# Low parts by a product with minus the identity, LayerNorm and block sums moved between engines

## The chip, the cores and the metric

One core of a Trainium2 chip runs the whole layer. The metric is the device time of one execution, in microseconds (us); lower is better. The kernel before takes 1218.13 us, the median of three runs (1217.9 to 1218.59).

## The reference

One decoder layer on 1024 tokens of width 1024, in float32:

```python
h = layer_norm(x, ln_in_g, ln_in_b)
proj = h @ w_in                       # q, k, v of two groups of 8 heads, 64 wide
sb = stick_breaking_attention(...)    # group 0, all earlier keys
sw = sliding_window_attention(...)    # group 1, last 128 keys, sinks, bias
merged = concat([rms_norm(sb, g0), rms_norm(sw, g1)])
h = layer_norm(ALPHA * h + merged @ w_out, ln1_g, ln1_b)
h = layer_norm(ALPHA * h + swiglu_ffn(h), ln2_g, ln2_b)
```

ALPHA is 2 to the power 1/4. An RMSNorm divides by a root mean square over 512 columns.

## The kernel before, in words

**Precision.** TensorE (PE) multiplies in a short float32 format (`fp32r`). Each operand is therefore split into a high part, rounded to that format, and a low part, the rest, and a product is three matmuls (`mm3`, L149). `split_w` (L105) splits what lies in SBUF: the high part on ScalarE (ACT), the low part by a subtraction on GpSimd (POOL). `split_ps` (L109) splits what lies in PSUM: the high part on ACT, the low part by a subtraction on VectorE (DVE), since POOL does not read PSUM.

**Stages, by the times of the profile.** The entry (0 to some 57 us): `entry(t)` (L282) normalizes the 8 tiles of 128 tokens, transposes each in two groups of four blocks into PSUM (tag `tr`, two banks), splits them into `xh` and `xl`, multiplies the tile by ALPHA and stores it to `h_dram` over ACT's DMA queue; the first projections and the first blocks of sliding-window attention run between the tiles. Then projections and attention, merged head pair by head pair, to some 489 us. Beside the last pair's attention (from some 385 us) run the four chunks of the first half of the output projection, `c1_steps` (L575), for the sliding-window group. From 489 to 574 us the second half runs for the other group: for each chunk `out_load` (L484) loads 512 rows by 256 tokens, splits them with `split_w` and forms squares on ACT and their sums over four blocks on POOL (L491, L492); `out_proj` (L495) sums the rest over the partitions by a product with ones (`pr`, L501), takes the power minus one half on POOL, and for each token tile runs 24 matmuls of 512 columns, which DVE scales and adds to `res` (L510); then `ln_apply` (L628) and `put_b` (L608), which transposes and splits tiles of 512 columns into the right operands of the feed-forward part (B11, B21 for the tokens of the first half; for those of the second half B22, T2, T3, T1, T4, which are sums and differences of blocks as in Strassen's scheme, L638 to L641). The chunks go in the order 0, 2, 1, 3. From 574 us the feed-forward part runs, with PE busy to the end.

**LayerNorm.** `ln_apply` (L128) has two forms. The fast one is three DVE instructions after the statistics (L131, and L134 twice). The other subtracts the mean on ACT (L141), multiplies on DVE (L142) and adds the bias on POOL (L144), each in two halves. The fast form serves tiles 0 to 2 of the entry and tile 7 of the second LayerNorm. The power for `rstd` is on POOL in both (L115).

**Order.** The order of each engine's queue is fixed when the program is built: the framework simulates the program and issues, on each engine, the ready instruction of the highest priority, program order first. An engine then works through its queue in that order. The DMA queue of SyncE (SP) carries all loads and the `h1_dram` stores.

## Time and profile before

| what | value |
|---|---|
| median of three runs | 1218.13 us |
| the profiled execution, its own time | 1216.92 us |
| its span, first to last instruction | 1215.1 us |
| PE / DVE / POOL / ACT busy share | 94% / 70% / 54% / 47% |
| mean granted TensorE clock | 0.974 |
| instructions | 17655 |

A group's row gives busy time, mean time of one instruction and the idle time of the engine just before, with what ended it. A wait names the engine that waited, the instruction that released it, the total, the number of times and the longest. A row of a timeline gives start, duration, engine, line, operation and tiles (output, arrow, inputs). PE is busy 94% over all, so the 6% in which it is not are in a few stretches, and those are looked at one by one.

### The profile page before, as it was taken

What the parts mean: (1) busy time and instruction counts of PE and PEld (TensorE: products, weight loads), DVE (VectorE), ACT (ScalarE), POOL (GpSimd) and SP (SyncE); (2) the same over time, 40 slices, a digit from 0 to 9 for tenths busy, and PEclk for the clock granted to TensorE, in tenths of its full rate; (3) what the DMA queues carried; (4) which work ended last, traced back from release to release, by engine and by line L of the source; (5) the groups of instructions that cost most, each with busy time, mean ns of one, the idle gap of its engine ahead of it and who ended that gap; (6) DMA issues with size and microseconds to landing.
All of it is one profiled execution on the core that took longest, in us unless ns stands there. A gap on an engine that the chain in (4) does not pass through costs nothing. (4 is left out here: it accounts for less than half of the span.)

```text
span 1215.1 us, 17655 instructions
## 1 busy us (share of the span) xinstructions
PE 1138.8 (94%) x6246; PEld 984.6 (81%) x6246; DVE 852.9 (70%) x1319; ACT 572.5 (47%) x1224; POOL 655.0 (54%) x620
## 2 busy tenths in 40 slices
PE   5698999999999898877999999999999999999997
PEld 3588999899998786765888888888888888888885
DVE  7876787788889896578765555555655438899735
ACT  4565677777768565233423322233222325445531
POOL 5614344566557875576886566665666612000584
PEclk9899999999999799987999999999999999999999
DMA  7213102020104635132333234332332239964431
GB/s 278 94 51 101 36 23 76 25 66 22 50 19 152 197 116 184 67 140 104 131 138 95 80 112 130 100 99 78 116 127 96 87 105 365 344 188 110 136 122 69
DMA packets 60053, 140.68 MB, mean 116 GB/s; under 512 B 7060, under 2 KB 18877, under 8 KB 59966
## 3 DMA queue, kind: packets, MB, share of 16 engines
q1 hardware_dynamic: 45406, 110.71, 28.4%
q10 hardware_dynamic: 14560, 28.85, 6.2%
q8 instruction: 49, 0.80, 0.3%
q14 instruction: 38, 0.31, 0.1%
HBM read 95.75 MB, written 41.17 MB: 113 GB/s over the span
## 5 line engine op out<-in xcount | busy, mean ns | idle before, releaser
L107 POOL TENSOR_TENSOR w<-s,w 128x512 fp32r<-128x512 f32 x88 | 123.6, 1407 | 120.1 <-ACT w L106 120.1
L154 PE MATMUL pp<-xh,whi 128*128 128x256 f32 x544 | 158.0, 291 | 0.5 <-DVE q L316 0.5
L154 PE MATMUL pp<-xh,wlo 128*128 128x256 f32 x544 | 156.9, 289 | 0.0
L154 PE MATMUL pp<-xl,whi 128*128 128x256 f32 x544 | 156.3, 287 | 0.0
L106 ACT CAST w<-s 128x512 fp32r<-128x512 f32 x88 | 54.4, 621 | 203.2 <-PE pgu L703 117.7
L776 PE MATMUL pd<-bhl,ahl 128*128 128x512 f32 x612 | 139.2, 389 | 0.0
L776 PEld LDWEIGHTS pd<-bhl,ahl 128*128 128x128 f32 x612 | 114.8, 188 | 24.2 <-DVE bhl L768 0.4
L735 DVE TENSOR_TENSOR t<-t,pgu 128x512 f32<-128x512 f32 x88 | 60.1, 683 | 96.2 <-PE pgu L703 95.9
L433 POOL TENSOR_TENSOR s<-s,s 128x127 f32<-128x127 f32 (+2 forms) x96 | 92.5, 968 | 37.7 <-DVE s L429 33.3
L154 PEld LDWEIGHTS pp<-xh,whi 128*128 128x128 f32 x544 | 105.5, 194 | 1.1 <-PE trx L290 0.6
L154 PEld LDWEIGHTS pp<-xh,wlo 128*128 128x128 f32 x544 | 105.3, 194 | 1.2
L154 PEld LDWEIGHTS pp<-xl,whi 128*128 128x128 f32 x544 | 105.4, 194 | 1.0
L768 POOL TENSOR_TENSOR ahl<-ar,ahl 128x512 fp32r<-128x512 f32 x12 | 16.2, 1354 | 134.8 <-ACT ahl L767 134.7
L429 DVE TENSOR_TENSOR_SCAN s<-s,brk 128x128 f32<-128x128 f32 (+1 forms) x64 | 74.8, 1175 | 11.3 <-ACT s L420 10.8
L110 ACT CAST at<-tra 128x256 fp32r<-128x256 f32 (+1 forms) x160 | 55.6, 356 | 53.1 <-DVE at L111 30.6
L767 ACT CAST ahl<-ar 128x512 fp32r<-128x512 f32 x63 | 39.1, 622 | 76.2 <-PE pd L776 48.8
L374 POOL TENSOR_TENSOR L<-L,rd 128x512 f32<-128x512 f32 (+1 forms) x32 | 30.9, 987 | 79.9 <-DVE rd L372 62.3
L111 DVE TENSOR_TENSOR at<-tra,at 128x256 fp32r<-128x256 f32 (+1 forms) x160 | 58.6, 383 | 18.3 <-ACT at L110 17.1
L107 POOL TENSOR_TENSOR w<-gr,w 128x512 fp32r<-128x512 f32 x44 | 61.1, 1402 | 2.0 <-ACT w L106 2.0
L703 PE MATMUL pgu<-B11h,w 128*128 128x512 f32 x176 | 59.3, 399 | 1.1 <-ACT w L106 1.1
L703 PE MATMUL pgu<-T4h,w 128*128 128x512 f32 x176 | 57.9, 390 | 0.0
L703 PE MATMUL pgu<-B22h,w 128*128 128x512 f32 x176 | 57.8, 389 | 0.0
(222 smaller groups left out, 3325.4 us busy)
## 6 DMA issues: line engine op xcount, KB each, us to landing
ar<-a_dram SPq DMA_DIRECT2D x73, 256.0 KB, 3.0
a_dram<-act ACTq DMA_DIRECT2D x33, 512.0 KB, 2.6
gr<-in_w_gu SPq DMA_DIRECT2D x24, 512.0 KB, 3.7
ur<-in_w_gu SPq DMA_DIRECT2D x23, 512.0 KB, 3.5
bq<-in_w_down SPq DMA_DIRECT2D x44, 256.0 KB, 5.2
raw<-in_w_sb SPq DMA_DIRECT2D x12, 512.0 KB, 3.5
h_dram<-x ACTq DMA_DIRECT2D x8, 512.0 KB, 3.5
m<-o_dram SPq DMA_DIRECT2D x32, 128.0 KB, 3.0
```

Source lines behind the costliest of these rows:

```text
L106: act.copy(hi, raw)
L107: pool.tensor_tensor(out=lo, in0=raw, in1=_f(hi), op=ALU.subtract)
L110: act.copy(hi, ps)
L111: dve.tensor_tensor(out=lo, in0=ps, in1=_f(hi), op=ALU.subtract)
L154: pe.matmul(ps, a, b, start=(i == 0), stop=(i == n - 1))
L374: pool.tensor_tensor(out=Ls[i], in0=Ls[i], in1=rd[:, 2 * i:2 * i + 2].unsqueeze(2).broadcast_to([P, 2, nk]), op=ALU.mult)
L429: dve.tensor_tensor_scan(s2[:, 0:w][:, ::-1], s2[:, 0:w][:, ::-1], brk[:, 512 - w:][:, ::-1] if last else zero.broadcast_to([P, w]), 1.0 i ...
L433: pool.tensor_tensor(out=s1[:, 0:m], in0=s1[:, 0:m], in1=s2[:, 1:m + 1], op=ALU.mult)
L703: pe.matmul(ps, a, b, start=(start and n == 0), stop=(stop and n == 11), skip_group_check=True)
L735: add = lambda out, x: dve.tensor_tensor(out=out, in0=x, in1=ps, op=ALU.add)
L767: act.copy(w[:, 0], src)
L776: pe.matmul(pd[t], x, y, start=(first and k == 0 and n == 0), stop=(end and k == KF - 1 and n == 2), skip_group_check=True)
```

## The change

The low part of a transposed operand is made in PSUM: the transposes are left open as an accumulation group, ACT copies the high part out, PE multiplies the high part by minus the identity into the same bank, and ACT copies what is left as the low part (`split_pe`). The product and the second copy of one split are issued after the transposes and first copy of the next (`pending`, `flush`). This serves the entry (16 splits) and `put_b` (28 calls; T4 in two halves, so 32 splits). From the tenth `put_b` on the transposes take turns between the PSUM tags `tr` and `av`. In `out_load` the low part goes from POOL to DVE, and the POOL sums go: four products with ones take the place of one. ALPHA is folded into the RMS factor and the epsilon, so that the entry's ACT pass over the tile goes. Entry tile 2 takes the slow form of LayerNorm, all tiles of the second LayerNorm the fast one. The sums and differences of `h` (L638, L639, L641) go from POOL to DVE. The entry's weight is loaded as one row and spread by a product with ones, as its bias is already, in place of a broadcast DMA.

```diff
@@ -90,6 +90,8 @@
     ident = cst.tile([P, P], F32, name="ident")
     make_identity(nc, ident)
+    negi = cst.tile([P, P], F32R, name="negi")
+    act.mul(negi, ident, -1.0)
     mhalf = cst.tile([P, 1], F32, name="mhalf")
     dve.memset(mhalf, -0.5)
     ones = cst.tile([P, 1], F32, name="ones")
@@ -110,11 +112,29 @@
         act.copy(hi, ps)
         dve.tensor_tensor(out=lo, in0=ps, in1=_f(hi), op=ALU.subtract)
+    def turn(ps, i, src):
+
+        pe.matmul(ps[:, i, :], src, ident, start=(i == 0), stop=False, is_transpose=True, skip_group_check=True)
+
+    def split_pe(pending, ps, hi, lo):
+
+        act.copy(hi, ps)
+
+        def finish():
+            pe.matmul(ps, negi, hi, start=False, stop=True, skip_group_check=True)
+            act.copy(lo, ps)
+        flush(pending)
+        pending.append(finish)
+
+    def flush(pending):
+        while pending:
+            pending.pop()()
+
     def rpow(dst, var, scale, eps):
         dve.tensor_scalar(out=var, in0=var, scalar1=scale, scalar2=eps, op0=ALU.mult, op1=ALU.add)
         pool.tensor_tensor(out=dst, in0=var, in1=mhalf, op=ALU.pow)
-    def ln_stats(xt, n=2):
+    def ln_stats(xt, n=2, eps=LN_EPS):
         bst = st.tile([P, n, 6], F32, tag=f"bst{n}", name="bst")
         w = D // n
         for i in range(n):
@@ -122,11 +142,11 @@
         mv = st.tile([P, 2], F32, tag="mv", name="mv")
         dve.bn_aggr(out=mv, in_=bst)
         rstd = st.tile([P, 1], F32, tag="rstd", name="rstd")
-        rpow(rstd, mv[:, 1:2], 1.0, LN_EPS)
+        rpow(rstd, mv[:, 1:2], 1.0, eps)
         return mv[:, 0:1], rstd
-    def ln_apply(dst, xt, g, b, fast=False):
-        mu, rstd = ln_stats(xt)
+    def ln_apply(dst, xt, g, b, fast=False, eps=LN_EPS):
+        mu, rstd = ln_stats(xt, 2, eps)
         if fast:
             dve.scalar_tensor_tensor(out=dst, in0=xt, scalar=mu, in1=g, op0=ALU.subtract, op1=ALU.mult)
             for i in range(2):
@@ -234,19 +254,20 @@
             sp.dma_start(xts[t][:, h], x[t * P:(t + 1) * P, h])
-    row = U([1, D], "row", F32)
-    sp.dma_start(row, ln_in[1].unsqueeze(0))
+    rows = [U([1, D], "row", F32) for i in range(2)]
+    for i in range(2):
+        sp.dma_start(rows[i], ln_in[i].unsqueeze(0))
     load_x(0)
     g_in = U([P, D], "g_in", F32)
     b_in = U([P, D], "b_in", F32)
-    bc_load(g_in, ln_in[0])
     load_x(1)
-    row1 = cst.tile([1, P], F32, name="row1")
+    row1 = bb.tile([1, P], F32, tag="oT", name="row1")
     dve.memset(row1, 1.0)
-    for h in (slice(0, 512), slice(512, D)):
-        ps = bps.tile([P, 512], F32, tag="pp", name="bc")
-        pe.matmul(ps, row1, row[:, h], start=True, stop=True)
-        act.copy(b_in[:, h], ps)
+    for i, dst in enumerate((g_in, b_in)):
+        for h in (slice(0, 512), slice(512, D)):
+            ps = bps.tile([P, 512], F32, tag=("pp", "av")[i], name="bc")
+            pe.matmul(ps, row1, rows[i][:, h], start=True, stop=True)
+            act.copy(dst[:, h], ps)
     sink = cst.tile([P, 8], F32, name="sink")
     nsink = cst.tile([P, 8], F32, name="nsink")
     sp.dma_start(sink, sinks.unsqueeze(0).broadcast_to([P, 8]))
@@ -281,15 +302,15 @@
     def entry(t):
         xt = xts.pop(t)
-        ln_apply(xt, xt, g_in, b_in, t < 3)
-        c, o = t // 2, (t % 2) * P
+        ln_apply(xt, xt, g_in, b_in, t < 2)
+        c, o, todo = t // 2, (t % 2) * P, []
         for g in range(2):
             ps = bps.tile([P, 4, P], F32, tag="tr", name="trx")
             for i in range(4):
                 k = 4 * g + i
-                pe.transpose(ps[:, i, :], xt[:, k * P:(k + 1) * P], ident)
-            split_ps(ps, xh[c][:, 4 * g:4 * g + 4, o:o + P], xl[c][:, 4 * g:4 * g + 4, o:o + P])
-        act.mul(xt, xt, ALPHA)
+                turn(ps, i, xt[:, k * P:(k + 1) * P])
+            split_pe(todo, ps, xh[c][:, 4 * g:4 * g + 4, o:o + P], xl[c][:, 4 * g:4 * g + 4, o:o + P])
+        flush(todo)
         act.dma_start(h_dram[t], xt)
     def xmul(w, c0, nc_):
@@ -486,11 +507,10 @@
         for i in range(4):
             sp.dma_start(m[:, i, :], o_dram[4 * g + i][:, c * 256:(c + 1) * 256])
         mh, ml = w_tiles((P, 4, 256))
-        split_w(m, mh, ml)
+        act.copy(mh, m)
+        dve.tensor_tensor(out=ml, in0=m, in1=_f(mh), op=ALU.subtract)
         act.activation(m, m, AF.Square)
-        pool.tensor_tensor(out=m[:, 0:2], in0=m[:, 0:2], in1=m[:, 2:4], op=ALU.add)
-        pool.tensor_tensor(out=m[:, 0], in0=m[:, 0], in1=m[:, 1], op=ALU.add)
-        return mh, ml, m[:, 0]
+        return mh, ml, m
     def out_proj(c, m, wo, acc):
         mh, ml, ss = m
@@ -498,9 +518,12 @@
             t = 2 * c + i
             tok = slice(i * P, (i + 1) * P)
             pr = bps.tile([P, 1], F32, tag="pp", name="pr")
-            pe.matmul(pr, ss[:, tok], ones, start=True, stop=True)
+            for k in range(4):
+                pe.matmul(pr, ss[:, k, tok], ones, start=(k == 0), stop=(k == 3))
             var = st.tile([P, 1], F32, tag="var", name="var")
-            dve.tensor_scalar(out=var, in0=pr, scalar1=1.0 / 512, scalar2=RMS_EPS, op0=ALU.mult, op1=ALU.add)
+
+            dve.tensor_scalar(out=var, in0=pr, scalar1=ALPHA ** 2 / 512, scalar2=ALPHA ** 2 * RMS_EPS,
+                              op0=ALU.mult, op1=ALU.add)
             r = st.tile([P, 1], F32, tag="r", name="r")
             pool.tensor_tensor(out=r, in0=var, in1=mhalf, op=ALU.pow)
             for d in range(2):
@@ -605,17 +628,20 @@
     t4 = [ws.tile([P, 2, 512], F32R, tag="raw", bufs=2, name="T4h") for i in range(2)]
     B["T4"] = (([(t4[0], 0), (t4[1], 2)], [t4[k // 2][:, k % 2] for k in range(4)]), btile(tl, "T4l"))
+    todo = []
+
+    turns = []
+
     def put_b(name, src, o):
-        ps = bps.tile([P, 4, P], F32, tag="tr", name="trh")
+        turns.append(name)
+        ps = bps.tile([P, 4, P], F32, tag="tr" if len(turns) < 10 else ("tr", "av")[len(turns) % 2], name="trh")
         for i in range(4):
-            pe.transpose(ps[:, i, :], src[:, i * P:(i + 1) * P], ident)
+            turn(ps, i, src[:, i * P:(i + 1) * P])
         (hw, _), (lw, _) = B[name]
         for hi, k0 in hw:
             n = hi.shape[1]
-            act.copy(hi[:, :, o:o + P], ps[:, k0:k0 + n])
-            dve.tensor_tensor(out=lw[0][0][:, k0:k0 + n, o:o + P], in0=ps[:, k0:k0 + n],
-                              in1=_f(hi[:, :, o:o + P]), op=ALU.subtract)
+            split_pe(todo, ps[:, k0:k0 + n], hi[:, :, o:o + P], lw[0][0][:, k0:k0 + n, o:o + P])
     order = (0, 2, 1, 3)
     ms = {c: out_load(0, c) for c in order[:2]}
@@ -625,7 +651,7 @@
         if n in (1, 2):
             ms[order[n + 1]] = out_load(0, order[n + 1])
         for t, h in out_proj(c, ms[c], wo, load_acc(c, acc_dram)):
-            ln_apply(h, h, g1, b1, t == NT - 1)
+            ln_apply(h, h, g1, b1, True, LN_EPS / ALPHA ** 2)
             sp.dma_start(h1_dram[t], h)
             o = (t % 4) * P
             if t < 4:
@@ -635,15 +661,16 @@
                 continue
             h0 = hs.pop(t - 4)
             tt = U([P, 2, 512], "tt", F32)
-            pool.tensor_tensor(out=h0[:, d0], in0=h[:, d0], in1=h0[:, d0], op=ALU.subtract)
-            pool.tensor_tensor(out=tt[:, 0], in0=h[:, d1], in1=h0[:, d0], op=ALU.subtract)
+            dve.tensor_tensor(out=h0[:, d0], in0=h[:, d0], in1=h0[:, d0], op=ALU.subtract)
+            dve.tensor_tensor(out=tt[:, 0], in0=h[:, d1], in1=h0[:, d0], op=ALU.subtract)
             dve.tensor_tensor(out=tt[:, 1], in0=h[:, d1], in1=h[:, d0], op=ALU.subtract)
-            pool.tensor_tensor(out=h0[:, d1], in0=h0[:, d1], in1=tt[:, 0], op=ALU.subtract)
+            dve.tensor_tensor(out=h0[:, d1], in0=h0[:, d1], in1=tt[:, 0], op=ALU.subtract)
             put_b("B22", h[:, d1], o)
             put_b("T2", tt[:, 0], o)
             put_b("T3", tt[:, 1], o)
             put_b("T1", h0[:, d0], o)
             put_b("T4", h0[:, d1], o)
+    flush(todo)
     RIGHT = {"P1": "B11", "P2": "B21", "P3": "B22", "P4": "T4", "P5": "T1", "P6": "T2", "P7": "T3"}
```

## Rows read from the trace of the kernel before

**Rows 1.** Windows: stretch, length; busy time (count) of PE, PEld, DVE, ACT, POOL; clock, DMA.

```profile
10.00:57.50 47.50, 27.84 (x165) 24.94 (x166) 44.15 (x71) 24.15 (x40) 32.46 (x22) 0.89 0.52 183
...
385.00:408.00 23.00, 16.06 (x80) 13.56 (x79) 21.18 (x27) 16.80 (x33) 22.46 (x18) 0.70 0.58 187
...
489.00:574.00 85.00, 67.86 (x320) 54.91 (x320) 61.16 (x114) 28.11 (x49) 54.58 (x50) 0.87 0.29 104
...
600.00:800.00 200.00, 200.00 (x884) 165.39 (x883) 117.93 (x124) 61.37 (x108) 135.57 (x98) 1.00 0.33 106
```

**Rows 2.** Waits of PE, 10 to 57.5 us.

```profile
PE trx L290 <- DVE x L134: 11.7, 2, 6.4
PE pv L325 <- DVE vr L322: 6.0, 1, 6.0
PE trx L290 <- DVE xl L111: 4.2, 1, 4.2
```

**Rows 3.** Groups of DVE, 10 to 57.5 us: count, busy, mean ns, idle before.

```profile
L142 DVE SCALAR_TENSOR_TENSOR x<-x,rstd,g_in 128x512 f32<-128x512 f32 x10 | 14.7, 1519 | 0.4 <-ACT x L141 0.4
...
L111 DVE TENSOR_TENSOR xl<-trx,xh 128x512 fp32r<-128x512 f32 x10 | 6.6, 675 | 0.1
...
L131 DVE SCALAR_TENSOR_TENSOR x<-x,mv,g_in 128x1024 f32<-128x1024 f32 x3 | 5.3, 1767 | 3.6 <-DMA g_in<-in_ln_in 3.6
```

**Rows 4.** Group of POOL, 10 to 57.5 us.

```profile
L144 POOL TENSOR_TENSOR x<-x,b_in 128x512 f32<-128x512 f32 x10 | 15.4, 1567 | 0.0
```

**Rows 5.** Waits of PE, 385 to 410 us.

```profile
PE tra L455 <- DVE at L111: 4.5, 2, 3.4
```

**Rows 6.** Groups of POOL, 385 to 410 us.

```profile
L107 POOL TENSOR_TENSOR wlo<-m,whi 128x1024 fp32r<-128x1024 f32 x3 | 7.1, 2379 | 0.0
L491 POOL TENSOR_TENSOR m<-m 128x512 f32<-128x512 f32 x3 | 4.3, 1438 | 0.0
L492 POOL TENSOR_TENSOR m<-m 128x256 f32<-128x256 f32 x2 | 3.4, 1722 | 0.0
```

**Rows 7.** Timeline of DVE around 377 and 387 us: start, duration, instruction.

```profile
377.20 1.26 DVE L429 TENSOR_TENSOR_SCAN s<-s,carry,zero 128x512 f32<-128x512 f32 x1
...
386.55 2.66 DVE L429 TENSOR_TENSOR_SCAN s<-s,carry,zero 128x512 f32<-128x512 f32 x1
```

**Rows 8.** Waits of PE, 489 to 574 us.

```profile
PE trh L612 <- DVE T2l L617: 3.0, 2, 1.9
...
PE trh L612 <- POOL res L144: 2.4, 4, 0.8
...
PE trh L612 <- POOL tt L639: 2.2, 1, 2.2
```

**Rows 9.** Group of DVE, 489 to 574 us.

```profile
L142 DVE SCALAR_TENSOR_TENSOR res<-res,rstd,g 128x512 f32<-128x512 f32 x14 | 11.3, 836 | 5.5 <-POOL rstd L115 3.7 <-ACT res L141 1.7
```

**Rows 10.** Group of POOL, 489 to 574 us.

```profile
L144 POOL TENSOR_TENSOR res<-res,b 128x512 f32<-128x512 f32 x14 | 19.8, 1433 | 10.5 <-DVE res L142 6.3 <-issue 3.0 <-PE pc L154 1.2
```

**Rows 11.** Timeline of the last tile's LayerNorm, 559 to 568 us.

```profile
559.87 0.74 DVE L510 SCALAR_TENSOR_TENSOR res<-pc,r,res 128x512 f32<-128x512 f32 x1
...
563.23 2.14 DVE L131 SCALAR_TENSOR_TENSOR res<-res,mv,g 128x1024 f32<-128x1024 f32 x1
563.68 0.58 ACT L616 CAST T2h<-trh 128x512 fp32r<-128x512 f32 x1 [2.31 <-PE trh L612]
...
566.49 1.40 DVE L134 SCALAR_TENSOR_TENSOR res<-res,rstd,b 128x512 f32<-128x512 f32 x2
```

**Rows 12.** Timeline of PE around 432 us: the product with ones, and what follows.

```profile
431.79 0.28 PE L501 MATMUL pr<-ones,m 128*128 128x1 f32 x2
431.92 0.31 PE L418 MATMUL z<-kd,q 128*128 128x128 f32 x1
```

**Rows 13.** Waits of PE, 135 to 385 us, on DVE's and ACT's halves of splits.

```profile
PE av L467 <- DVE at L111: 2.3, 4, 0.8
PE av L466 <- ACT at L110: 1.3, 1, 1.3
```

## The prediction

> **What bounds the kernel now.** I read the windows of the whole span first, to find where PE is not busy. From 600 to 800 us PE is busy all the time, 884 matmuls in 200 us, or 0.226 us each; there only fewer matmuls would help, and the change touches none of them. Three stretches differ [rows 1]. In the entry, 10 to 57.5 us, PE is busy 27.8 of 47.5 us, while DVE is busy 44.2. From 385 to 408 us PE is busy 16.1 of 23 us, with POOL at 22.5 and DVE at 21.2, and the granted clock is 0.70: part of it ran at the lower level, 1.2 GHz. From 489 to 574 us PE is busy 67.9 of 85 us at 0.87. The idle time of the three is 19.7, 6.9 and 17.1 us, and that is what the change can reach.
>
> Next I read, for each stretch, what PE waits for. In the entry it is DVE: 11.7 us for the LayerNorm's last instruction, 6.0 us for a copy that stands in DVE's queue behind such work, 4.2 us for a low part [rows 2]. From 385 us on it is DVE's half of the attention's splits, 4.5 us [rows 5], which hangs on scans and POOL products. In the last stretch POOL's results are named with 4.6 us, and low parts that free a PSUM bank, such as T2l with 3.0 [rows 8].
>
> All terms are made against the profiled execution, 1216.92 us (span 1215.1, 1.8 us around it). It lies 1.2 us under the median of 1218.13, so I add the sum to the median.
>
> **A, the entry.** Ten low parts of 0.675 us leave DVE by 57.5 us, 6.6 us [rows 3]. Tile 2 goes from the fast form to the slow one: nothing to 1.8 us of DVE time, its L131; I take 0.9. The weight: DVE sat idle 3.6 us for the broadcast load [rows 3]. With products the weight is early, but the bias now comes third and fourth in PE's queue, so it becomes the late operand; between nothing and 3.6 us I take 1.1. DVE is relieved by 8.6 us. Against that, tile 2 gives POOL two adds of 1.567 us [rows 4], 3.1 us, and DVE waits for POOL's power and PE for its adds. Forecast -5.5, bounds 0 and -8.6. ACT loses 8 ALPHA passes of 1024 columns and gains 16 copies of 512, which is even; the ALPHA passes stood ahead of the stores on its queue and nobody waited for them. The 16 products with minus the identity are 16 x 0.226 = 3.6 us; PE's 19.7 idle us cover them, and if the entry becomes tight they are paid. One 512 KB load leaves SP's queue and a 4 KB one comes; the tiles behind it can only land earlier.
>
> **B, 385 to 408 us.** Of POOL's 22.5 busy us, 7.1 + 4.3 + 3.4 = 14.8 are `out_load`'s subtractions and sums [rows 6], and they stand in POOL's queue between the products that the attention waits for. All of that goes. DVE gains three subtractions of 1024 columns, an operation that the trace does not show there: two halves of 512 took 1.40 us beside an idle POOL, and the L131 of the same size 2.14 us beside a busy one [rows 11], so 4.2 to 6.4 us. It gets time back: the same scan took 1.26 us at one place and 2.66 us beside POOL's subtraction [rows 7], and with two thirds of POOL's work gone most scans should be the short kind. What DVE has queued behind a subtraction that waits for ACT's high part is the attention's low parts, for which PE waits; the subtractions of POOL waited for the same copy, but with less behind them. Forecast -5 of the 6.9 idle us and the slow clock, bounds +2 (DVE stays full) and -9.
>
> **C, matmuls where PE is full.** The product with ones becomes four, for 8 tiles in two groups: 48 more. One takes two passes, and the next matmul starts 0.13 us after it [rows 12]: 48 x 0.13 = 6.2 us. In the last stretch B11 and B21 of four tiles are made between dense projections: 8 x 0.226 = 1.8. Together +8.0; bounds 6 and 12.5, the latter if the other 16 full and 8 half products of `put_b`, 4.5 us, were not covered by the waits around them.
>
> **D, 489 to 574 us.** PE's four waits for the bias add on POOL, 2.4 us, go, as the add does [rows 8]. So does the wait for POOL's difference, 2.2 us, but four DVE instructions take its place, at some 0.7 each (half of the 1.40); I count half, 1.1. The waits for a bank I count at nothing: `put_b` gets four banks in place of two, but at the end of each half PE then waits for the next loads, which SP issues behind the LayerNorm's stores (L629 stands before them in the program). So what counts there is the LayerNorm of the last tile of each half. The slow form runs over ACT (two passes, each about the 0.58 of a copy of its size [rows 11]), DVE at 0.836 [rows 9] and POOL at 1.433 [rows 10]: first pass, first product, two adds, 0.58 + 0.84 + 2.87 = 4.3 us. The fast one is 1.4 + 1.4 = 2.8 without POOL beside it: -1.5. The last tile has the fast form already; from its L510 at 559.87 to its end at 567.89 it took 8.0 us, with L131 stretched to 2.14 and three low parts and a POOL power behind POOL's differences inside. Without low parts (3 x 0.68) and stretch (0.7), but with the four DVE differences (2.8) of the tile before possibly inside, it is 5.3 to 8.1; I take -2. Sum -7.0, bounds -2 and -10. DVE as a whole is not loaded more: 24 low parts of 0.68 and 8 of half size, some 19 us, leave against seven fast forms in place of slow ones (7 x (2.8 - 1.7) = 7.7) and 12 differences (8.4). ACT gains as many copies as DVE loses subtractions, and is busy 28 of 85 us [rows 1].
>
> **E, waiting for the copy.** PE now waits inside a split for ACT's high copy, which no row shows. At least 0: other matmuls stand between. At most the whole copy, 0.58 us, at each of 48 products: 27.8 us. The nearest rows are the attention's products, which also read what ACT and DVE have just split: from 135 to 385 us PE waited 3.6 us for them in all [rows 13]. I take +1.
>
> Sum: -5.5 - 5 + 8.0 - 7.0 + 1 = **-8.5**, 1208.4 for the profiled execution and **1209.6** at the median.
>
> **Rivals.**
>
> 1. All stalls close: A -8.6, B -9, D -10, C +8, E 0, together -19.6, **1198.5**. For it: POOL and DVE are lightened exactly where PE waits. Against it: loads on SP and the entry's POOL adds stay. Chance 0.20.
>
> 2. Evened out: the entry stays tied to POOL (A -3), DVE stays full at 385 us (B -1), D -5, with C and E as above: 0, **1218**. Chance 0.12.
>
> 3. DVE and POOL block each other. The moved instructions have two SBUF inputs; the low parts that leave had one in PSUM, and all took about 0.675 us [rows 3], however busy POOL was, while L131 took 1.767 in the mean and L142 1.519 of some 0.7. If each moved instruction waits out a POOL one wherever POOL is busy, A is 0 and B +2, with D -5: +6, **1224**. It decides from the point where the locked time of B's three subtractions and the scans exceeds POOL's freed 14.8 us. Chance 0.13.
> The Trainium skill (SBUF — State Buffer, Who interferes with whom) says the same: a DVE instruction with two SBUF inputs and a GpSimd instruction that reads SBUF exclude each other for their whole length. By that rule the three subtractions of B would each cost one POOL sum more, and the sum above would come to about -4; the two lengths of the scan agree with it.
>
> 4. PE stands still at each product: PE's queue is worked in order, so a product that waits for ACT holds every matmul behind it. If ACT's copy is always just ahead, E is 27.8 in place of 1: +18.3, **1236.4**; with more than 16 of 48 exposed (9.5 / 0.58) the gain is gone. Against it [rows 13], and that each product is issued behind the next transposes. Chance 0.07.
> The Trainium skill (TensorE: Matmul & The Clock Gate, Step-by-step: what each phase is for) has matmuls keep program order, with only weight loads pulled ahead; PE's waits for ACT and DVE in this trace agree.
>
> **How the numbers follow.** The forecast has 0.48, the rivals 0.20, 0.12, 0.13 and 0.07. About 0.2% (2.4 us) is what a measurement of this kernel can tell from no change. Faster: 0.48 + 0.20 = 0.68; same 0.12; slower 0.13 + 0.07 = 0.20. The range goes from 1198.5, the first rival with half its chance below, to 1222, which leaves out the fourth and part of the third: some 0.2.
>
> **What would show it.** Right: the first projection starts some 4 us earlier, and PE's idle time before its first full stretch shrinks by 5 or more; from 385 to 408 us POOL is no longer full and scans of 512 columns are near 1.26; the product with ones shows 128 instructions; no PE wait names POOL's `res`. Wrong: waits of PE on ACT's copy at the new products of over 5 us in all (rival 4); the subtractions of `out_load` on DVE at over 2 us, with the scans as long as before (rival 3); or the stretches 489 to 574 and 385 to 489 us grown by the added matmuls with the same idle time.

## The result, and the profile after

The changed kernel takes 1199.56 us, the median of four runs (1198.88 to 1200.13), against 1218.02 (1216.38 to 1218.59) for the kernel before in the same comparison: a ratio of 0.9862, 95% interval 0.9844 to 0.9879. The medians lie 18.5 us apart; by the ratio, with which the variants below are compared, it is 16.8 us of 1218. The forecast was 8.5 us less; the measured time lies at the low end of the range, 1 us above what the first rival gave (1198.5). The profiled execution took 1199.59 us, span 1197.9. PE is busy 96% of it, DVE 70%, ACT 49%, POOL 49%, the mean granted clock is 0.986.

To see where the time came from I cut both spans at the same events of PE: the first projection's matmul, the last matmul of the entry's last projection strip, the last projection, the last output-projection matmul of the sliding-window group, the last one of the other group, and the first matmul of the feed-forward part. A window's columns are those of [rows 1]. The kernel before:

```profile
0.00:23.00 23.00, 8.91 (x23) 4.35 (x23) 16.06 (x32) 7.51 (x10) 8.44 (x12) 1.00 0.77 268
23.00:112.20 89.20, 72.30 (x531) 69.14 (x530) 72.04 (x144) 56.25 (x140) 41.41 (x31) 0.92 0.32 104
112.20:387.00 274.80, 269.13 (x2139) 259.85 (x2138) 220.03 (x392) 193.94 (x499) 140.73 (x198) 1.00 0.16 48
387.00:475.70 88.70, 81.15 (x431) 68.56 (x430) 77.42 (x111) 51.87 (x117) 66.40 (x80) 0.92 0.47 158
475.70:558.90 83.20, 67.93 (x317) 55.04 (x316) 52.76 (x107) 31.83 (x55) 53.15 (x48) 0.90 0.32 114
558.90:574.00 15.10, 7.21 (x35) 5.16 (x33) 12.77 (x19) 5.09 (x11) 11.24 (x9) 0.70 0.44 157
```

The same windows of the kernel after:

```profile
0.00:22.00 22.00, 13.34 (x25) 5.91 (x26) 16.83 (x37) 9.94 (x15) 9.56 (x14) 1.00 0.70 235
22.00:107.10 85.10, 76.46 (x561) 71.65 (x560) 61.31 (x129) 58.97 (x154) 43.70 (x34) 0.98 0.32 111
107.10:378.40 271.30, 267.20 (x2126) 259.37 (x2125) 218.72 (x387) 192.92 (x492) 139.20 (x197) 0.99 0.17 50
378.40:465.20 86.80, 83.55 (x479) 72.08 (x478) 71.98 (x116) 51.64 (x118) 48.30 (x67) 0.96 0.49 162
465.20:543.90 78.70, 72.48 (x380) 60.72 (x379) 56.88 (x100) 30.53 (x58) 15.26 (x16) 0.93 0.36 126
543.90:556.80 12.90, 10.14 (x59) 6.94 (x57) 8.25 (x14) 10.90 (x25) 1.46 (x1) 1.00 0.45 151
```

The stages are 1.0, 4.1, 3.5, 1.9, 4.5 and 2.2 us shorter, 17.2 in all; from the first feed-forward matmul to the end both take 641.1. What to read in each row is its length minus PE's busy time, the time that PE is idle. In the second stage PE does 30 instructions more and idles 8.6 us in place of 16.9. In the fourth it does 48 more and idles 3.2 in place of 7.5. In the last two 87 more instructions fit into 6.7 us less: the idle time falls from 23.2 to 9.0 us. In the last, where PE was busy 7.21 of 15.10 us at a granted clock of 0.70, the lower level was there for part of the time; after, with 10.14 of 12.90 us busy, it is 1.00.

The waits of PE in the entry and the first projections, 0 to 107 us (for [rows 2]; columns: total, times, longest):

```profile
PE trx L117 <- DVE x L154: 4.0, 1, 4.0
PE trx L117 <- ACT xl L125: 2.6, 2, 1.9
PE trx L124 <- ACT xh L121: 2.5, 4, 0.9
```

The waits for the LayerNorm are a third of the 11.7 us they were; the wait for a DVE low part has become one for ACT's copies, 5.1 us in all. In the kernel before, the largest waits of the last stretch were for low parts on DVE that free a PSUM bank; [rows 8] shows the first of these:

```profile
PE trh L612 <- DVE T2l L617: 3.0, 2, 1.9
PE trh L612 <- DVE T3l L617: 2.6, 1, 2.6
PE trh L612 <- DVE T4l L617: 2.6, 2, 1.3
```

The waits of the kernel after from 465 to 557 us (for [rows 8]):

```profile
PE pr L522 <- DVE res L533: 2.7, 1, 2.7
PE av L487 <- ACT at L112: 1.5, 1, 1.5
...
PE trh L117 <- ACT T1h L121: 0.5, 1, 0.5
PE trh L124 <- ACT T4h L121: 0.4, 1, 0.4
PE trh L124 <- ACT B22h L121: 0.3, 1, 0.3
```

No wait names POOL's `res` or its differences, no wait names a DVE low part, and at the new products (L124) PE waits 0.7 us here. The window from 385 to 408 us, with the columns of [rows 1]:

```profile
385.00:408.00 23.00, 21.86 (x114) 18.53 (x115) 18.47 (x34) 15.57 (x37) 9.99 (x16) 0.88 0.69 223
```

PE is idle for 1.1 us of it, where it was 6.9, and POOL's busy time has fallen from 22.5 to 10.0. The groups of DVE from 385 to 408 us (for [rows 6, 7]; columns: busy, mean ns, idle before):

```profile
L450 DVE TENSOR_TENSOR_SCAN s<-s,brk 128x128 f32<-128x128 f32 (+3 forms) x7 | 5.3, 754 | 0.1
...
L502 DVE SCALAR_TENSOR_TENSOR wo<-raw,gT,wo 128x1024 fp32r<-128x1024 f32 x4 | 5.1, 1280 | 1.7 <-ACT wo L501 1.7
...
L511 DVE TENSOR_TENSOR wlo<-m,whi 128x1024 fp32r<-128x1024 f32 x1 | 1.2, 1211 | 0.0
```

The subtraction of 1024 columns takes 1.21 us here and 1.48 at 409 us, less than the 2.14 that was its upper bound. A scan of 512 columns at 401.95 us takes 1.22. The last tile's LayerNorm (for [rows 11]: start, duration):

```profile
544.74 0.74 DVE L533 SCALAR_TENSOR_TENSOR res<-pc,r,res 128x512 f32<-128x512 f32 x1
...
547.03 1.28 DVE L151 SCALAR_TENSOR_TENSOR res<-res,mv,g 128x1024 f32<-128x1024 f32 x1
548.75 1.41 DVE L154 SCALAR_TENSOR_TENSOR res<-res,rstd,b 128x512 f32<-128x512 f32 x2 [0.44 <-POOL rstd L135]
550.08 0.69 DVE L664 TENSOR_TENSOR res<-res 128x512 f32<-128x512 f32 x1
```

It ends 5.4 us after its L533 (548.75 + 1.41 - 544.74), against 8.0 before; L131 (now L151) is back from 2.14 to 1.28 us.

### The profile page after: what moved, and what is told of

Same layout as the page of the kernel before. It is cut to its first block, busy times and chain, and to the rows that moved or that the text cites. A ratio compares the mean times of both kernels' runs of the same rounds, so it can differ in the third digit from the quotient of the medians.

```text
span 1197.9 us, 17900 instructions
## 1 busy us (share of the span) xinstructions
PE 1154.2 (96%) x6394; PEld 997.9 (83%) x6394; DVE 837.7 (70%) x1291; ACT 581.3 (49%) x1255; POOL 591.8 (49%) x572
## 5 line engine op out<-in xcount | busy, mean ns | idle before, releaser
L450 DVE TENSOR_TENSOR_SCAN s<-s,brk 128x128 f32<-128x128 f32 (+1 forms) x64 | 69.4, 1089 | 12.0 <-ACT s L441 11.2
L441 ACT ACTIVATE s<-z 128x128 f32<-128x128 f32 (+2 forms) x96 | 47.6, 498 | 23.9 <-PE z L440 15.7
```

Of the source, the lines that this page charges most:

```text
L441: act.activation(s2[:, 0:w], ps, AF.Sigmoid, scale=-SCALE)
L450: dve.tensor_tensor_scan(s2[:, 0:w][:, ::-1], s2[:, 0:w][:, ::-1], brk[:, 512 - w:][:, ::-1] if last else zero.broadcast_to([P, w]), 1.0 i ...
```

## The experiments

All twelve start from the changed kernel and undo or alter one part. The third column is the variant's ratio minus 0.9862, times 1218 us; its uncertainty combines the half widths of both intervals. A positive number is what undoing that part costs. Each variant's queues are ordered anew by the framework, so a variant measures its edit together with the order that comes with it. The stage lengths come from one profile each; seven profiles whose code is the same up to there end the second stage between 106.7 and 110.1 us, so a difference under some 3 us in that stage proves nothing by itself. Other lengths are steadier where the code is the same: these seven end the third stage between 377.9 and 380.0 us; nine profiles have a fourth stage of 86.5 to 87.3 us (a tenth, entry_dve_low, 92.2); and from its end to the end of the program six take 732.2 to 734.3 us, the kernel before 739.4.

| variant | median us, ratio [95%] | against the change, us | stage lengths, us |
|---|---|---|---|
| the change | 1199.56, 0.9862 [0.9844, 0.9879] | | 22.0 85.1 271.3 86.8 78.7 12.9 |
| entry_old | 1210.39, 0.9953 [0.9935, 0.9971] | +11.1 ± 3.1 | 22.6 91.6 274.7 87.0 79.5 13.5 |
| entry_dve_low | 1201.73, 0.9884 [0.9866, 0.9902] | +2.7 ± 3.1 | 22.2 84.5 273.2 92.2 77.5 12.1 |
| entry_alpha | 1208.88, 0.9943 [0.9922, 0.9965] | +9.9 ± 3.4 | 22.1 91.3 271.3 86.5 78.5 12.6 |
| alpha_dve | 1204.40, 0.9900 [0.9884, 0.9916] | +4.6 ± 2.9 | 21.2 86.1 275.5 87.2 78.9 12.7 |
| gin_dma | 1204.71, 0.9917 [0.9894, 0.9940] | +6.7 ± 3.5 | 24.1 88.2 271.7 86.7 78.4 12.9 |
| put_dve_low | 1204.88, 0.9897 [0.9878, 0.9917] | +4.3 ± 3.2 | 23.0 85.5 270.1 86.8 80.7 16.1 |
| tr_only | 1205.32, 0.9905 [0.9878, 0.9932] | +5.2 ± 3.9 | 21.5 85.2 271.5 86.8 80.1 12.0 |
| at_once | 1199.57, 0.9854 [0.9835, 0.9874] | -1.0 ± 3.2 | 21.2 85.5 270.2 87.3 77.3 12.2 |
| ln_pool | 1203.30, 0.9885 [0.9867, 0.9904] | +2.8 ± 3.1 | 22.6 85.5 269.8 87.2 80.2 13.6 |
| load_pool | 1201.31, 0.9871 [0.9850, 0.9891] | +1.1 ± 3.3 | 22.7 87.0 269.9 88.8 80.4 11.9 |
| sums_pool | 1197.25, 0.9844 [0.9822, 0.9866] | -2.2 ± 3.4 | 22.9 85.2 271.2 83.4 80.9 13.1 |
| sums_g1 | 1198.75, 0.9854 [0.9836, 0.9873] | -1.0 ± 3.1 | 23.1 87.0 269.9 83.4 81.1 12.7 |

### The entry

**entry_dve_low.** The entry's low parts go back to DVE; the 16 products go.

```diff
-                turn(ps, i, xt[:, k * P:(k + 1) * P])
-            split_pe(todo, ps, xh[c][:, 4 * g:4 * g + 4, o:o + P], xl[c][:, 4 * g:4 * g + 4, o:o + P])
+                pe.transpose(ps[:, i, :], xt[:, k * P:(k + 1) * P], ident)
+            split_ps(ps, xh[c][:, 4 * g:4 * g + 4, o:o + P], xl[c][:, 4 * g:4 * g + 4, o:o + P])
```

> Changed kernel with the entry's 16 low parts made by VectorE again, all else as changed. If VectorE's queue set the entry's length (term A), the gain of the entry goes: some +5 us, 1204.5, the last projection of the entry's fourth strip back near 112 us from 107, VectorE over 90% busy from 10 to 57 us. Rival: the early weight and the missing ALPHA pass made the gain: within 1 us of 1199.6.

Measured: +2.7 ± 3.1 us, and the second stage is not longer (84.5 us). PE idles more in it, 11.7 us (84.5 - 72.79) against 8.6, but has 3.6 us of products less to do, and 12 matmuls more stand behind its end (2134 and 483 in the next two stages in place of 2126 and 479). The third stage ends at 379.9 us, within the spread. So the exchange of DVE's low parts for products, on which the prediction built 6.6 us, is not shown to shorten the entry by itself. The profile is of the slowest of six runs (1205.97 us), and its long fourth stage (92.2 us) lies where the edit changes nothing; why is not shown.

**entry_alpha.** Only the ALPHA pass comes back.

```diff
         flush(todo)
+        act.mul(xt, xt, ALPHA)
         act.dma_start(h_dram[t], xt)
...
-            dve.tensor_scalar(out=var, in0=pr, scalar1=ALPHA ** 2 / 512, scalar2=ALPHA ** 2 * RMS_EPS,
+            dve.tensor_scalar(out=var, in0=pr, scalar1=1.0 / 512, scalar2=RMS_EPS,
...
-            ln_apply(h, h, g1, b1, True, LN_EPS / ALPHA ** 2)
+            ln_apply(h, h, g1, b1, True)
```

> Changed kernel with only the ALPHA pass (8 x 1.06 us on ScalarE) back in the entry. As predicted nobody waits for it: last projection of the fourth strip within 1.5 us of 107.1, total within 1.5 us of 1199.6. Rival: ScalarE now carries the low parts too, the pass stands ahead of them, and that stage grows by 3 us or more.

Measured: +9.9 ± 3.4 us, the largest effect of any single edit; the second stage is 6.2 us longer, and the third ends at 384.7 us. PE's waits up to 113 us, where those of after stand above:

```profile
PE trx L124 <- ACT xh L121: 6.6, 4, 3.9
PE trx L117 <- ACT xl L125: 4.2, 3, 2.8
PE pv L347 <- DVE vr L344: 3.8, 1, 3.8
```

And ACT's timeline at the longest of these:

```profile
37.29 1.33 ACT L161 ACTIVATE x<-x,nmu 128x512 f32<-128x512 f32 x2 [6.21 <-DVE nmu L158]
...
39.28 2.56 ACT L161 ACTIVATE x<-x,nmu 128x512 f32<-128x512 f32 x4
41.75 0.56 ACT L121 CAST xh<-trx 128x512 fp32r<-128x512 f32 x1
42.22 1.05 ACT L314 ACTIVATE x<-x 128x1024 f32<-128x1024 f32 x1
43.18 0.56 ACT L121 CAST xh<-trx 128x512 fp32r<-128x512 f32 x1
```

The high copy, for which PE stands with an open split (its transposes start at 33.19 us), comes behind six first passes of the slow LayerNorm, and an ALPHA pass stands between it and the next. ACT sat idle 6.21 us just before, since the first of those passes waited for DVE. It is the fixed order of its queue that holds PE up here, not its load. In the changed kernel the copy at this place runs before any of these passes, the first of which starts at 37.26 us:

```profile
34.77 0.58 ACT L121 CAST xh<-trx 128x512 fp32r<-128x512 f32 x1 [1.71 <-PE trx L117]
```

DVE's queue is ordered otherwise too: the copy `vr`, for which PE waits 3.8 us, starts at 37.54 behind the statistics of three tiles, and at 33.63 in the changed kernel, ahead of two of them. So the 9.9 us are the price of the pass together with the orders that the framework made with it; how much of it is the pass's own time on ACT (8 of some 1.05 us) is not shown.

**alpha_dve.** The ALPHA pass comes back together with DVE's low parts.

```diff
+        act.mul(xt, xt, ALPHA)
...
-            split_pe(todo, ps, xh[c][:, 4 * g:4 * g + 4, o:o + P], xl[c][:, 4 * g:4 * g + 4, o:o + P])
+            split_ps(ps, xh[c][:, 4 * g:4 * g + 4, o:o + P], xl[c][:, 4 * g:4 * g + 4, o:o + P])
```

> Changed kernel with the ALPHA pass back on ScalarE and the entry's low parts back on VectorE. The ALPHA pass alone put 6 us on the entry, with ScalarE carrying the low parts and TensorE waiting 6.6 us for its high copies. If the two compete for ScalarE, the pass costs under 2 us beside low parts on VectorE: fourth strip's last projection by 109, total 1203. Rival: the pass costs 6 whatever else ScalarE does: 113, total 1208.

Measured: +4.6 ± 2.9. Beside entry_dve_low (+2.7) the pass costs 1.9 ± 2.9 us; beside low copies on ACT it costs 9.9, which is 7.9 ± 4.5 us more. Read the other way, with the pass in place the low parts by products cost 5.2 ± 3.3 us (0.9943 against 0.9900), and without it they gain 2.7 ± 3.1. So the two edits belong together. The timeline above fits the reason that each ACT copy of a split is now a step of PE's path, with the pass between two such steps; that the order of the queues alone does it is a rival that these runs do not separate.

**gin_dma.** Only the weight comes by broadcast DMA again.

```diff
...
+    bc_load(g_in, ln_in[0])
     load_x(1)
...
-    for i, dst in enumerate((g_in, b_in)):
-        for h in (slice(0, 512), slice(512, D)):
-            ps = bps.tile([P, 512], F32, tag=("pp", "av")[i], name="bc")
-            pe.matmul(ps, row1, rows[i][:, h], start=True, stop=True)
-            act.copy(dst[:, h], ps)
+    for h in (slice(0, 512), slice(512, D)):
+        ps = bps.tile([P, 512], F32, tag="pp", name="bc")
+        pe.matmul(ps, row1, row[:, h], start=True, stop=True)
+        act.copy(b_in[:, h], ps)
```

> Changed kernel with only the weight's broadcast DMA back. Predicted worth 1.1 us: first projection at 23 in place of 22.0, total 1200.7. Rival: the 512 KB load delays the tiles and weights behind it in the queue, and the fourth strip's last projection comes 4 us later, 111, total 1203.

Measured: +6.7 ± 3.5 us; the first projection starts at 24.1 us in place of 22.0, the next stage is 3.1 us longer, and the third ends at 384.0 us. DVE's timeline of this variant:

```profile
8.99 1.28 DVE L151 SCALAR_TENSOR_TENSOR x<-x,mv,g_in 128x1024 f32<-128x1024 f32 x1 [3.44 <-DMA g_in<-in_ln_in]
...
11.74 1.28 DVE L141 BATCH_NORM_STATS2 bst<-x 128x6 f32<-128x512 f32 x2
```

And of the kernel after:

```profile
7.73 1.29 DVE L141 BATCH_NORM_STATS2 bst<-x 128x6 f32<-128x512 f32 x2 [1.68 <-DMA x<-in_x]
8.93 1.27 DVE L151 SCALAR_TENSOR_TENSOR x<-x,mv,g_in 128x1024 f32<-128x1024 f32 x1
```

The first instruction that uses the weight starts no earlier (8.93 against 8.99). What is earlier is the second tile: its statistics run at 7.73, inside the time that DVE spent idle for the weight, in place of 11.74. The 512 KB of the broadcast stand ahead of that tile's load in SP's queue: it takes 7.7 us to landing there and 5.3 in the changed kernel, which is some 10.3 and 7.7 us on the clock of the span. The rest of the 4.0 us is the order of DVE's queue, where the first tile's three instructions on weight and bias come first. PE's waits for the LayerNorm (L154) in the entry are 10.2 us in place of 4.0. The prediction priced the weight's wait and left the load behind it at nothing.

**entry_old.** All four entry edits are undone (low parts, ALPHA pass and weight, and `t < 2` back to `t < 3`).

```diff
-        ln_apply(xt, xt, g_in, b_in, t < 2)
+        ln_apply(xt, xt, g_in, b_in, t < 3)
...
```

> Changed kernel with all four edits of the entry undone: low parts on VectorE, ALPHA pass on ScalarE, weight by broadcast DMA, tile 2 in the fast form; the second LayerNorm and out_load as changed. If these four hold the entry's whole gain, the last projection of the entry's fourth strip is back at 112 us (107.1 changed, 106.7 with only the low parts undone), and the total is some 1205. Rival: the entry's gain came with the new order of the queues whatever the edit: below 109 us, total 1200 to 1202.

Measured: +11.1 ± 3.1 us, so the four entry edits make some 11 of the 16.8 us, and all the rest some 5.7 (a ratio of 0.9953 [0.9935, 0.9971] is left: 3.5 to 7.9 us). The single effects of the three (2.7, 9.9, 6.7) sum to 19.3 and not to this, as the pass costs far less beside low parts on DVE (alpha_dve). From alpha_dve to this one, the weight and tile 2's form are worth 6.5 ± 2.9 us. The third stage, which no edit touches, is 3.4 us longer again, with 2139 matmuls in place of 2126: 1.9 of that is PE's busy time (269.11 against 267.20), work of the entry that slips past the boundary, and the rest waits.

### The transposes of the second LayerNorm

**put_dve_low.** `put_b` splits on ACT and DVE as before, in the changed kernel's four banks.

```diff
-            turn(ps, i, src[:, i * P:(i + 1) * P])
+            pe.transpose(ps[:, i, :], src[:, i * P:(i + 1) * P], ident)
...
-            split_pe(todo, ps[:, k0:k0 + n], hi[:, :, o:o + P], lw[0][0][:, k0:k0 + n, o:o + P])
+            split_ps(ps[:, k0:k0 + n], hi[:, :, o:o + P], lw[0][0][:, k0:k0 + n, o:o + P])
```

> Changed kernel with put_b's low parts made by VectorE again, with the changed PSUM banks. If the low parts on VectorE delay the LayerNorms (term D): +3 us, 1202.5, the stretch from the last sliding-window projection to the first feed-forward matmul near 95 us in place of 91.6. Rival: only the four banks and the moved LayerNorm matter there, and the 32 products (24 x 0.226 + 8 x 0.113 = 6.3 us of TensorE) are pure cost: -4 us, 1195.5.

Measured: +4.3 ± 3.2 us; in the profile the last two stages are 5.2 us longer, and from the end of the fourth to the end of the program it is 737.8 us, against 732.7 for the change and 739.4 before. PE's waits there:

```profile
PE trh L640 <- DVE res L154: 4.4, 1, 4.4
...
PE trh L640 <- DVE tt L665: 1.7, 2, 1.1
```

With the low parts in DVE's queue the LayerNorm and the differences come later: PE waits 4.4 us for the last LayerNorm, where it waited for no L154 at all. From its L533 at 547.65 to its end at 555.77 us that LayerNorm takes 8.1 us, with five low parts inside, one of half size, in place of 5.4. Here the low parts on DVE cost more than the products.

**tr_only.** The transposes keep to the two banks of tag `tr`.

```diff
-        ps = bps.tile([P, 4, P], F32, tag="tr" if len(turns) < 10 else ("tr", "av")[len(turns) % 2], name="trh")
+        ps = bps.tile([P, 4, P], F32, tag="tr", name="trh")
```

> Changed kernel with put_b in the two banks of tag tr alone. The prediction counted the waits for a bank at nothing: within 1 us of 1199.6. Rival: a bank is now held through two copies and a product, so with two banks TensorE waits for ScalarE in the last stretch, which grows by 2 to 4 us: 1202 to 1204.

Measured: +5.2 ± 3.9 us, and in a place that the stage lengths hide. The first feed-forward matmul starts at 557.1 us, as in the changed kernel, but from there to the end it takes 647.0 us in place of 641.1 (640.3 to 642.6 in all other profiles). PE's timeline shows why:

```profile
557.07 0.50 PE L730 MATMUL pgu<-B11h,w 128*128 128x512 f32 x1 [0.31 <-ACT w L108]
...
568.95 0.60 PE L117 MATMUL trh<-ident,res 128*128 128x128 f32 x4
...
577.07 0.28 PE L124 MATMUL trh<-T4h,negi 128*128 128x256 f32 x1
```

Transposes go on to 569 us and products to 577, among the feed-forward matmuls; in the changed kernel the last transposes start at 553.03 and the last product at 562.02. PE has 20 instructions more behind its first feed-forward matmul (4.7 us more busy time, 1.3 more idle). Ahead of it the length is the same though some 20 instructions fewer stand there. PE waits there for a low copy that frees a bank, a wait that the changed kernel does not show, and from 465 to 545 us the granted clock is lower than the 0.93 of after:

```profile
PE trh L117 <- ACT T1l L125: 2.2, 1, 2.2
...
465.30:545.40 80.10, 74.54 (x369) 61.76 (x368) 57.29 (x100) 28.80 (x53) 15.28 (x16) 0.89 0.35 123
```

From the end of the fourth stage to the end of the program this variant takes 739.1 us, the kernel before 739.4. So with two banks, as with DVE's low parts (737.8), nearly all of the 6.7 us that the change gains there is gone: it needs both parts.

**at_once.** The product is written down straight after its own high copy, not behind the next transposes.

```diff
-        flush(pending)
-        pending.append(finish)
+        finish()
```

> Changed kernel with each product with minus the identity and its copy written down straight after the high copy, not behind the next transposes. By rival 4 of the prediction (matmuls in order, each waiting 0.58 us for the copy) up to 48 x 0.58 = 28 us are lost where nothing stands between: the total rises by over 5 us, with over 5 us of TensorE waits for ScalarE's high copies. Against it: the framework orders ready work by itself, and other matmuls stand between anyway: within 2 us of 1199.6.

Measured: -1.0 ± 3.2, no difference that shows. PE's wait at the entry's products is

```profile
PE trx L124 <- ACT xh L121: 4.9, 4, 2.2
```

in place of 2.5 us (2.8 to 4.3 in the six other profiles with the changed entry), but the stages are no longer. So it is not shown to matter that the product is written down behind other transposes; in PE's queue, as the framework orders it, transposes or other matmuls often stand between all the same. For the fourth rival, which had 0.58 us at each of 48 products, even this order has 0.3 us in the mean (4.9 over the entry's 16).

### LayerNorm, subtractions and sums

**ln_pool.** The slow LayerNorm for tiles 0 to 6, and the three differences on POOL.

```diff
-            ln_apply(h, h, g1, b1, True, LN_EPS / ALPHA ** 2)
+            ln_apply(h, h, g1, b1, t == NT - 1, LN_EPS / ALPHA ** 2)
...
-            dve.tensor_tensor(out=h0[:, d0], in0=h[:, d0], in1=h0[:, d0], op=ALU.subtract)
-            dve.tensor_tensor(out=tt[:, 0], in0=h[:, d1], in1=h0[:, d0], op=ALU.subtract)
+            pool.tensor_tensor(out=h0[:, d0], in0=h[:, d0], in1=h0[:, d0], op=ALU.subtract)
+            pool.tensor_tensor(out=tt[:, 0], in0=h[:, d1], in1=h0[:, d0], op=ALU.subtract)
...
-            dve.tensor_tensor(out=h0[:, d1], in0=h0[:, d1], in1=tt[:, 0], op=ALU.subtract)
+            pool.tensor_tensor(out=h0[:, d1], in0=h0[:, d1], in1=tt[:, 0], op=ALU.subtract)
```

> Changed kernel with the slow LayerNorm for seven tiles of the second LayerNorm and with the three differences on GpSimd again. By term D the undoing costs most of its 7 us: 1205 to 1206.5, with TensorE's waits for GpSimd's res and tt back (2.4 and 2.2 us). Rival: the low parts by products and the banks made the gain of that stretch: within 1 us of 1199.6.

Measured: +2.8 ± 3.1. The last three stages of the table are 0.4, 1.5 and 0.7 us longer, which agrees, but the interval holds nothing: it is not shown that this part pays by itself.

**load_pool.** Subtraction and sums of `out_load` back on POOL, and one product with ones.

```diff
-        act.copy(mh, m)
-        dve.tensor_tensor(out=ml, in0=m, in1=_f(mh), op=ALU.subtract)
+        split_w(m, mh, ml)
...
+        pool.tensor_tensor(out=m[:, 0:2], in0=m[:, 0:2], in1=m[:, 2:4], op=ALU.add)
+        pool.tensor_tensor(out=m[:, 0], in0=m[:, 0], in1=m[:, 1], op=ALU.add)
...
-            for k in range(4):
-                pe.matmul(pr, ss[:, k, tok], ones, start=(k == 0), stop=(k == 3))
+            pe.matmul(pr, ss[:, 0, tok], ones, start=True, stop=True)
```

> Changed kernel with out_load's subtraction and block sums on GpSimd again and one product with ones. By terms B (-5) and C (+6.2) the undoing costs 5 and gives back 6.2: -1 us, 1198.5; the idle time of TensorE from 378 to 400 us comes back, with GpSimd full there. Rival: GpSimd's queue at that place is worth more than the products: +5 us, 1204.5.

Measured: +1.1 ± 3.3 us in all, while the mechanism stands out. The window from 386 to 409 us, with the columns of [rows 1]:

```profile
386.00:409.00 23.00, 18.52 (x85) 15.69 (x86) 19.70 (x28) 14.36 (x32) 21.20 (x22) 0.70 0.54 173
```

DVE's groups in it, which after had at 5.1 and 5.3 us:

```profile
L502 DVE SCALAR_TENSOR_TENSOR wo<-raw,gT,wo 128x1024 fp32r<-128x1024 f32 x4 | 7.6, 1906 | 1.9 <-ACT wo L501 1.9
L450 DVE TENSOR_TENSOR_SCAN s<-s,brk 128x128 f32<-128x128 f32 (+3 forms) x6 | 6.9, 1150 | 0.0
```

And PE's longest wait from 380 to 469 us:

```profile
PE tra L476 <- DVE at L113: 4.5, 2, 3.4
```

POOL is full again, the granted clock is at 0.70 again (0.88 after), the same L502 takes 1906 ns in place of 1280, and PE waits 4.5 us for the attention's low parts, as in [rows 5]. Both times of L502 are with two SBUF inputs on DVE.
The Trainium skill (SBUF — State Buffer, Who interferes with whom) has such an instruction and a GpSimd one that reads SBUF exclude each other; these means agree. In the fourth and fifth stage PE idles 16.1 us in place of 9.5, and the fourth is at 88.8 us, the 88.7 of the kernel before. Against that the added products are gone: PE is busy 153.1 us in place of 156.0, at a lower granted clock (0.92 and 0.89 against 0.96 and 0.93). So gain and price of this part nearly cancel.

**sums_pool and sums_g1.** Only the sums go back to POOL, with one product; the subtraction stays on DVE. In sums_g1 this is done for the sliding-window group alone, beside the attention.

```diff
+        pool.tensor_tensor(out=m[:, 0:2], in0=m[:, 0:2], in1=m[:, 2:4], op=ALU.add)
+        pool.tensor_tensor(out=m[:, 0], in0=m[:, 0], in1=m[:, 1], op=ALU.add)
...
-            for k in range(4):
-                pe.matmul(pr, ss[:, k, tok], ones, start=(k == 0), stop=(k == 3))
+            pe.matmul(pr, ss[:, 0, tok], ones, start=True, stop=True)
```

> Changed kernel with out_load's block sums on GpSimd again and one product with ones, the subtraction staying on VectorE. By term C 48 products of 0.13 us leave TensorE where it is full: -6.2, less what GpSimd's sums bring back of the stall after 378 us (2 of the 4.3 us that came back with sums and subtraction): 1195 to 1196. Rival: the sums alone hold up the attention's products on GpSimd: the stall comes back whole and the total is 1199 or more.

> Changed kernel with block sums on GpSimd and one product for the four chunks that run beside the attention only; the last stretch keeps its four products. With sums on GpSimd everywhere the stretch beside the attention took 83.4 us in place of 86.8 and the last one 80.9 in place of 78.7. Kept where it helped: -3.1 (24 x 0.13) to -3.4 us, 1196.3, ratio to before 0.983. Rival: the 3.4 us were a single profile's luck: 1199.6, ratio 0.986.

Measured: -2.2 ± 3.4 and -1.0 ± 3.1: neither beats the change for certain. PE's busy time in the fourth and fifth stage gives the price of the products: 156.0 us with all, 153.0 without the 24 of one group, 149.2 without all 48, so 0.125 and 0.14 us each, the 0.13 of the prediction. But the idle time goes the other way, 9.5, 11.5 and 15.1 us. In sums_pool PE's longest waits from 463 to 556 us are these:

```profile
PE av L487 <- ACT at L112: 4.1, 1, 4.1
PE pr L523 <- DVE res L534: 3.1, 1, 3.1
PE trh L124 <- ACT T4h L121: 1.6, 2, 1.0
```

Most of what fewer matmuls save is waited out at the next dependence. In sums_g1 the fourth stage is 3.4 us shorter and the fifth 2.4 longer, with 22 matmuls more in it (402 for 380): work that had filled the fourth.

## Why the prediction was right and where it was wrong

The direction was right, and so were the places; the size was short by half, and that the range held the time, 1 us from its end, was in part luck (see the rivals). By the stages of the two profiles, with C's matmuls where they run:

| part | forecast | measured | 
|---|---|---|
| A, to the last projection | -5.5 | -8.6 |
| B with 24 of C's 48 products | -5 + 3.1 = -1.9 | -1.9 |
| D, E and the rest of C | -7.0 + 1 + 3.1 + 1.8 = -1.1 | -6.7 |
| all | -8.5 | -17.2 |

- **A failed in its reason and in size.** "Ten low parts of 0.675 us leave DVE by 57.5 us, 6.6 us" was the largest step, and entry_dve_low measured 2.7 ± 3.1 in its place, the products paid. "The weight ... between nothing and 3.6 us I take 1.1" measured 6.7 ± 3.5 (gin_dma; 6.5 ± 2.9 with tile 2), since the load that leaves SP's queue lets the next tile land 2.6 us earlier: the text said that the tiles "can only land earlier" and gave it no price. That "the ALPHA passes ... nobody waited for them" was near with low parts on DVE (1.9 ± 2.9, alpha_dve against entry_dve_low) and wrong for the changed kernel, where keeping them, with the queue order that comes of it, would cost 9.9. Undone together the four edits cost 11.1 us, the double of the forecast.
- **B and C came out as worked out.** From 385 to 408 us PE's idle time falls from 6.9 to 1.1 us and the granted clock rises from 0.70 to 0.88, with L511 at 1.21 to 1.48 us, and the products take 0.125 to 0.14 us each. load_pool and sums_pool show both halves, and that they nearly cancel.
- **D was the larger miss.** "The waits for a bank I count at nothing" is the step that failed: two banks in place of four cost 5.2 ± 3.9 us (tr_only), although the stretch ahead of the feed-forward part is no longer for it. The trace before had named such waits with 8.2 us (T2l, T3l, T4l). The other half of the same step is the low parts of `put_b`: I called DVE "not loaded more" and gave the exchange no gain beyond three low parts of the last tile, but put_dve_low costs 4.3 ± 3.2, since the last LayerNorm waits behind them. The two effects do not add up: either one undone leaves 0.3 to 1.6 of the 6.7 us. The last tile's LayerNorm became 2.6 us shorter, forecast 2.
- **E** was small, as forecast, but not 1: PE waits 2.5 + 0.7 = 3.2 us at the new products; at_once, with 4.9 in the entry alone, is no slower within ± 3.2 us.
- **The signs.** The first did not come: the first projection starts 1.0 us earlier, not 4. The others did: PE idles 17.3 us before 107.1 in place of 31.0 before 112.2, POOL is busy for 10.0 of 23 us, a scan of 512 columns takes 1.22 us, the products with ones are 128 instructions, and no wait names POOL's `res`.
- **Rivals.** The first, with all stalls closing, is what came, though by other terms: its A of -8.6 is met up to the last projection, its B of -9 is not. The second and fourth are refuted, the fourth by the 3.2 us of waits in place of 27.8. The third is refuted as a loss: its mechanism exists (load_pool), but the change takes POOL's instructions out of DVE's way. The first came to pass because three gains that stood at zero or near it (the load behind the weight, the banks, the low parts of `put_b`) all fell on the same side; that is luck, and not the reason that rival gave.
- **Still open.** The parts of 2.8 us or less (ln_pool, entry_dve_low, sums) are within their uncertainty. The slow form of entry tile 2 was not tried alone. What of the 9.9 us of entry_alpha is the pass and what the order of the queues is open. Why waits in the untouched third stage are 1.6 us shorter is not shown.

## What to carry to other kernels

When a step moves from one engine's queue to another's, price what stands behind the removed instruction (the next load, the next split, the next bank), not only its own wait; a zero in the sum needs a row as much as a number does. Edits that put an engine on the critical path and edits that clear that engine's queue have to be judged together: taking the pass over ALPHA out was worth 1.9 ± 2.9 us with low parts on DVE and 9.9 ± 3.4 with them on PE and ACT. And where PE is nearly full, matmuls that replace work elsewhere are paid in full in busy time, but cutting them again may only turn them into waits.

## What the runs showed that I had not expected

A shortage of PSUM banks left little trace where it arose: in tr_only there is one wait of 2.2 us, but the stretch ahead of the feed-forward part is as long as ever, and 5.9 us appear behind it, as transposes and products between matmuls of a stage that was taken to be a fixed 641 us. And the low part by a product cost less than its count of instructions suggests. The products of 512 columns last 394 to 503 ns in the second LayerNorm and up to 795 in the entry,

```profile
L124 PE MATMUL trx<-xh,negi x16: 394/488/795, 12.9 to 86.3; 128*128 128x512 f32 x16
```

(min, median, max), and in the last two stages 87 more PE instructions than before fit into 6.7 us less time.
